# A hybrid encoder layer on one core: branch B's convolution and product placed earlier, attention's end and the first norm factor shifted

## The chip, the core and the metric

The kernel runs on one core of one Trainium2 chip. Time is device time in microseconds (us) of one execution; the median of several runs is compared. "Row" below means a line of the profile, taken of one execution by the hardware profiler. The engines are PE (TensorE matmul, with PEld its weight loads), DVE (VectorE), ACT (ScalarE), POOL (GpSimd) and SP (SyncE, which here only issues DMAs).

## The reference, cut to what matters

One layer over 1024 prompt tokens and 32 sample tokens, model width 1024, all in float32; each of five branches is 256 wide:

```python
xn = rmsnorm(x, norm1_g)
z = xn @ w_in                       # columns split among the branches
# A: gMLP
ga = gelu(za); ua = ga[..., :W]; va = layernorm(ga[..., W:], a_ln_g, a_ln_b)
oa = ua * gmlp_spatial(va, a_ws, a_bs)
# B: Conformer convolution module
b_in = zb[..., :W] * sigmoid(zb[..., W:])
b_ext = concat([hist_b, b_in])
ob = silu(layernorm(causal_dwconv(b_ext, b_conv_w) + b_conv_b, b_ln_g, b_ln_b))   # 31 taps
# C: gated short convolution (3 taps)     D: multi-scale pooling     E: cross-attention into 256 memory tokens
branches = (oa, ob, oc, od, oe)
merged = sum_n sigmoid(xn @ w_gate[n] + b_gate[n]) * (branches[n] @ w_branch[n])
x = x + merged @ w_out
x = x + (silu(hn @ w_ffn_gate) * (hn @ w_ffn_up)) @ w_ffn_down     # hn = rmsnorm(x, norm2_g)
```

`rmsnorm` divides by the root of a token's mean square. The outputs are the normed x, the memory's keys and values, and the last rows of several branches.

## The kernel before

**Layout.** Activations are feature-major: a tile has 128 features as partitions and tokens along the free axis. The tokens are two column groups `c` of 528 (two halves of 264). A float32 operand is kept as a pair of reduced-precision parts (`split`: the high part by ACT, L149, the low part by DVE, L150), and `product` (L167) makes three matmuls of each pair, so a projection of one 128-wide output tile for one group is 48 matmuls of 264 columns.

**Stages, in program order.** Memory keys and values; the query projections (which use x scaled by the norm's gain alone, `xn`); branch B's input projections; branch C's; C's gate (`gated`); A's `ua` (feature-major); A's `va` (token-major, eight tiles of 128 tokens and one of 32); branch D's input (`place`); the branch products by `branch()` for e, c, a, d, which are copied by ACT into a temporary `pb` (L1021) and written to DRAM (`pb_d`) by ACT's queue; 20 gate pairs of seven products each; the output product `wo`; the feed-forward part.

**The norm's factor.** `x_squares(c)` adds up squares of x in `r1[c]` on ACT and DVE (L370). `factors` sums them over features with matmuls to a column (`fm`, L289), takes the inverse root on ACT and DVE (`fv`, `ft`, `fr`), builds diagonal tiles (L313), and `spread` gives them back along the tokens with matmuls (`fs`, L326). `x_factor(c)` is the first half, `x_spread(c)` the second. `again` rescales x into `xs`.

**Background work.** A `runner` wraps a generator; each call with a cost steps it until the costs that it yields are used up. `att_bg` runs the attention's steps, `b_bg` runs `whole_b`: `conv_b` (30 taps on DVE and one on ACT for each of two feature halves and three token pieces: 120 taps of 512 columns, 60 of 32), then for the sample rows and each group `norm_b` (a layer norm over features: `lm`, `fm`, `fs` on PE) and `own_b` (the product of B's branch: weights `wr` loaded by SP in tiles of 128 columns, split into `wp`, twelve matmuls in two halves, copied by ACT to a temporary `pb`, L786, and written by POOL's queue). Whatever is left of `b_bg` when gate pair 15 of 20 is reached is run out at once by `b_bg.drain()`.

**What sets the order.** The framework schedules each engine's list from the program with its dependences, so a call's place decides only roughly where its instructions stand. Buffers come from pools: temporaries (`temp`) share one pool of four 528-column buffers; `by`, the convolution's accumulator, is one of them. After the attention the PSUM pool has two single banks and three double ones. In `own_b`:

```python
raw = fpool.tile([P, 2, P], F32, name=f"wr{c}_{mt}", tag="wr", bufs=1)
```

and beside the gates each of the first 16 pairs gives `b_bg` a step of 0.95 at each of its seven products.

## Time and profile before

| | us |
|---|---|
| three runs | 1716.91, 1719.30, 1724.15 |
| median | 1719.3 |
| the profiled execution | 1714.05 |
| its span on the core | 1712.0 |

| engine | busy us in the span | share |
|---|---|---|
| PE | 1655.8 | 97% |
| DVE | 1086.8 | 63% |
| ACT | 706.7 | 41% |
| POOL | 129.3 | 8% |

Times in rows are counted from the start of the span. The three runs of the table and the profiled execution are four executions of one program; the profiled one is the shortest of them.

### The profile page before, as it was taken

What the parts mean: (1) busy time and instruction counts of PE and PEld (TensorE: products, weight loads), DVE (VectorE), ACT (ScalarE), POOL (GpSimd) and SP (SyncE); (2) the same over time, 40 slices, a digit from 0 to 9 for tenths busy, and PEclk for the clock granted to TensorE, in tenths of its full rate; (3) what the DMA queues carried; (4) which work ended last, traced back from release to release, by engine and by line L of the source; (5) the groups of instructions that cost most, each with busy time, mean ns of one, the idle gap of its engine ahead of it and who ended that gap; (6) DMA issues with size and microseconds to landing.
All of it is one profiled execution on the core that took longest, in us unless ns stands there. A gap on an engine that the chain in (4) does not pass through costs nothing.

```text
span 1712.0 us, 31925 instructions
## 1 busy us (share of the span) xinstructions
PE 1655.8 (97%) x13246; PEld 1631.5 (95%) x13246; DVE 1086.8 (63%) x1946; ACT 706.7 (41%) x1314; POOL 129.3 (8%) x225
## 2 busy tenths in 40 slices
PE   8999989999999999969989999999999999999997
PEld 7999979988999999969989999999999999999997
DVE  7766674867997675535666686666666666242446
ACT  6546762555444554434443343333333334131221
POOL 1110000000111111111010000000000003000000
PEclk9999989999999999979999999999999999999999
DMA  8531102665556656635682212222222228331012
GB/s 291 171 128 43 38 13 77 223 219 207 164 159 157 147 139 166 169 109 139 201 327 82 83 38 79 84 75 88 78 85 75 75 88 300 128 110 63 29 38 102
DMA packets 77152, 213.55 MB, mean 125 GB/s; under 512 B 10544, under 2 KB 18288, under 8 KB 77008
## 3 DMA queue, kind: packets, MB, share of 16 engines
q1 hardware_dynamic: 39392, 113.80, 20.3%
q0 software_dynamic: 24848, 78.05, 15.6%
q10 hardware_dynamic: 12768, 19.67, 3.1%
q8 instruction: 103, 1.69, 0.4%
q14 instruction: 41, 0.34, 0.1%
HBM read 143.80 MB, written 67.70 MB: 124 GB/s over the span
## 4 chain that ended last, share of the span: by engine, by line
PE 80%; DMA 6%; issue 6%; DVE 4%; ACT 2%; POOL 1%; SPq 0%; ACTq 0%; POOLq 0%; DVEq 0%
PE sa L167 24%; PE dn L167 13%; PE sy L167 11%; PE z L167 9%; PE sx L167 6%; PE wo L167 5%; PE pb L167 3%; PE dq L167 2%; DMA fr<-in_w_gate 2%; PE va L167 2%; DMA pb_d<-pb 1%; DMA x<-in_x 1%; DMA mg_d<-acc 1%; PE fs L326 1%; DMA mr<-mg_d 1%
## 5 line engine op out<-in xcount | busy, mean ns | idle before, releaser
L167 PE MATMUL sa<-x,s 128*128 128x264 f32 x1968 | 252.1, 284 | 0.5 <-ACT p L1190 0.5
L167 PEld LDWEIGHTS sa<-x,s 128*128 128x128 f32 x1968 | 244.0, 188 | 0.9 <-ACT p L1190 0.7
L167 PE MATMUL dn<-hp,hl 128*128 128x264 f32 x1824 | 222.3, 284 | 0.0
L167 PEld LDWEIGHTS dn<-hp,hl 128*128 128x128 f32 x1824 | 222.1, 188 | 0.1
L149 ACT ACTIVATE s<-s 128x512 fp32r<-128x512 f32 x164 | 102.8, 631 | 143.7 <-PE sa L167 62.1
L149 ACT ACTIVATE hl<-raw 128x512 fp32r<-128x512 f32 (+1 forms) x128 | 76.8, 615 | 201.5 <-PE dn L167 130.5
L150 DVE TENSOR_TENSOR s<-s,s 128x512 fp32r<-128x512 f32 x164 | 112.4, 687 | 46.0 <-ACT s L149 45.4
L150 DVE TENSOR_TENSOR hl<-raw,hl 128x512 fp32r<-128x512 f32 (+1 forms) x128 | 84.3, 671 | 76.6 <-ACT hl L149 76.2
L167 PE MATMUL sa<-t,a 128*128 128x264 f32 x984 | 127.2, 285 | 3.2 <-DVE p L1205 3.2
L150 DVE TENSOR_TENSOR a<-fr,a 128x512 fp32r<-128x512 f32 x123 | 84.5, 688 | 71.7 <-ACT a L149 71.4
L167 PE MATMUL sy<-x,s 128*128 128x264 f32 x984 | 127.0, 285 | 0.0
L167 PEld LDWEIGHTS sa<-t,a 128*128 128x128 f32 x984 | 122.5, 189 | 4.5 <-DVE p L1205 4.5
L167 PEld LDWEIGHTS sy<-x,s 128*128 128x128 f32 x984 | 122.8, 189 | 0.0
L167 PE MATMUL z<-xs,hl 128*128 128x264 f32 x960 | 120.0, 285 | 0.5 <-ACT va_dec L841 0.5
L167 PEld LDWEIGHTS z<-xs,hl 128*128 128x128 f32 x960 | 117.9, 188 | 0.8 <-ACT va_dec L841 0.7
L149 ACT ACTIVATE a<-fr 128x512 fp32r<-128x512 f32 x123 | 77.8, 633 | 72.7 <-issue 57.8
L674 DVE SCALAR_TENSOR_TENSOR by<-b_ext,vec,by 128x512 f32<-128x512 f32 (+1 forms) x174 | 99.4, 578 | 4.7 <-ACT by L669 2.2
L167 PE MATMUL wo<-mg,hl 128*128 128x264 f32 x768 | 96.5, 288 | 3.0 <-DVE mg L150 3.0
L167 PEld LDWEIGHTS wo<-mg,hl 128*128 128x128 f32 x768 | 95.4, 191 | 3.5 <-DVE mg L150 3.5
L1436 DVE TENSOR_TENSOR y<-y,dn 128x528 f32<-128x528 f32 x40 | 28.0, 702 | 82.4 <-PE dn L167 82.3
L167 PE MATMUL pb<-br,hl 128*128 128x264 f32 x576 | 74.0, 289 | 6.3 <-ACT pb L1021 6.3
L167 PEld LDWEIGHTS pb<-br,hl 128*128 128x128 f32 x576 | 72.0, 192 | 7.4 <-ACT pb L1021 7.4
(298 smaller groups left out, 2732.7 us busy)
## 6 DMA issues: line engine op xcount, KB each, us to landing
pi<-pb_d SPq DMA_DIRECT2D x40, 528.0 KB, 5.4
fr<-in_w_gate SPq DMA_DIRECT2D x40, 512.0 KB, 4.1
pb_d<-pb ACTq DMA_DIRECT2D x64, 264.0 KB, 3.3
mg_d<-p POOLq DMA_DIRECT2D x48, 264.0 KB, 4.9
h_d<-h POOLq DMA_DIRECT2D x22, 528.0 KB, 3.0
hu<-h_d POOLq DMA_DIRECT2D x22, 528.0 KB, 8.8
fr<-in_w_fg SPq DMA_DIRECT2D x21, 512.0 KB, 3.5
fr<-in_w_fu SPq DMA_DIRECT2D x21, 512.0 KB, 3.6
```

The lines of the kernel that those rows point to most:

```text
L149: nc.scalar.activation(hl[:, 0], src, AF.Copy)
L150: nc.vector.tensor_tensor(hl[:, 1], src, hl[:, 0].bitcast(F32), op=ALU.subtract)
L167: nc.tensor.matmul(out, w(wi), rhs, start=start and i == 0, stop=stop and i == n - 1, skip_group_check=not (start and stop),)
L326: nc.tensor.matmul(ps[q][:, t0 : t0 + n] if narrow else ps[:, q, t0 : t0 + n], ones[: rows[i]], diag[: rows[i], q * Q + t0 : q * Q + t0 + ...
L674: nc.vector.scalar_tensor_tensor(dst, tap(k), col("bw", 31 * j + k), y, op0=ALU.mult, op1=ALU.add)
L1436: nc.vector.tensor_tensor(quarters(dst), quarters(dst), ps, op=ALU.subtract)
```

## The change

Seven edits stand in the diff. The first factor's `fm` and `fs` matmuls are called one product later, and those of the second group too. The attention's steps are larger (1.5 and 1.6 instead of 1.4 and 1.5), and its calls in `va` go. B's convolution gets its own buffer, is defined before branch C and is stepped beside C, `gated`, `ua`, `va` and `place`, with larger costs, and no longer beside the branches c, a and d. `own_b` loads its weights two tiles ahead and splits them one ahead, and yields less per half tile; `norm_b` is called inside it. The constants of A's layer norm and spatial bias leave the start of the program for a unit buffer that SP fills after `ua`. D's scaling moves from DVE to ACT, and the splits of a branch's parts are made for one group at a time and at later calls. The first output tile of `wo` takes the second group first.

```diff
@@ constants
-    ln_a = const.tile([P, 2, BW], F32, name="ln_a")
-    bs_b = const.tile([P, 2, P], F32, name="bs_b")
...
-        nc.sync.dma_start(ln_a[:, 0], a["a_ln_g"].partition_broadcast(P))
-        nc.sync.dma_start(ln_a[:, 1], a["a_ln_b"].partition_broadcast(P))
-        nc.sync.dma_start(bs_b, a["bs_b"])
@@ query projections, in the loop over c and j
+            if c == j == 1:
+                x_factor(0)
             if j == 0:
                 x_squares(c)
-            if c == 1:
-                (x_factor, x_spread)[j](0)
@@ branch B's projections, in the loop over j and c
             ps = projected(wb_[0], c, xn)
             if j == c == 0:
-                x_factor(1)
+                x_spread(0)
             else:
+                if j == 0:
+                    x_spread(1)
                 again()
...
             ps = projected(wb_[1], c, xn)
             if j == c == 0:
-                x_spread(1)
+                x_factor(1)
@@ conv_b, defined before branch C now, as are norm_b, own_b, whole_b and b_bg
-                y = temp("by")[:, :n]
+                y = bpool.tile([P, SEQ // 2], F32, name=f"by{j}_{t0}", tag="by")[:, :n]
...
-                    yield 0.7 if n > DEC else 0.1
+                    yield 0.9 if n > DEC else 0.15
@@ own_b
+        raws_ = {}
+
+        def load(mt):
+            if mt < KT:
+                raws_[mt] = fpool.tile([P, 2, P], F32, name=f"wr{c}_{mt}", tag="wr", bufs=2)
+                nc.sync.dma_start(
...
+        def weights(mt):
+            w = fpool.tile([P, 2, 2, P], F32R, name=f"wp{c}_{mt}", tag="wp", bufs=2)
+            split(w, raws_.pop(mt))
+            load(mt + 2)
+            return w
+
+        load(0)
+        load(1)
+        yield from norm_b(c)
+        ahead = weights(0)
+        yield
         for mt in range(KT):
...
+            w, out = ahead, temp("pb")
+            if mt < KT - 1:
+                ahead = weights(mt + 1)
...
-                yield 2
+                yield 0.9
@@ branch C, gated, ua
-                    att_bg(1.4)
+                    att_bg(1.5)
+                    b_bg(1.8)
...
-        project(gated, xs, lambda: att_bg(1.4))
+        project(gated, xs, lambda: (att_bg(1.6), b_bg(1.8)))
...
-        project(ua_evac, xs, lambda: (att_bg(1.5), b_bg(1.4)))
+        project(ua_evac, xs, lambda: (att_bg(1.6), b_bg(1.8)))
@@ after ua, and in the loop over va's tiles
+    a_const = unit(F32, "a_const")
+    ln_a, bs_b = a_const[:, :, :BW], a_const[:, :, BW : BW + P]
+    nc.sync.dma_start(ln_a[:, 0], a["a_ln_g"].partition_broadcast(P))
...
-        if i % 2 == 0:
-            att_bg()
+        b_bg(1.8)
@@ place
-        project(place, xs, lambda: (a_bg(), b_bg(2)))
+        project(place, xs, lambda: (a_bg(), b_bg(1.8)))
@@ mix_d
-                nc.vector.tensor_scalar(quarters(br[3][c][:, j]), ps, col("ds", j), None, op0=ALU.mult)
+                nc.scalar.activation(quarters(br[3][c][:, j]), ps, AF.Copy, scale=col("ds", j))
@@ beside the branches; to_parts yields after each group
-        if i == 6:
-            to_parts(2)
-        else:
-            b_bg(0.7)
+        if i in (9, 11):
+            c_parts()
+        elif i > 11:
+            b_bg(0.9)
...
-        b_bg(0.4)
+        if i in (11, 13):
+            a_parts()
...
-        if i > 3:
-            b_bg(0.4)
...
-    branch(3, lambda i: (comb(0.5), b_bg(0.4)))
+    branch(3, lambda i: comb(0.5))
@@ gates
-            hooks = {m: lambda: b_bg(0.95) for m, _ in ORDER}
+            hooks = {m: b_bg for m, _ in ORDER}
@@ wo
-        for c in range(NC):
+        for c in (1, 0) if mt == 0 else (0, 1):
```

**The first factor on PE.** In these rows z is a projection's product (here of the queries, then of branch B), `fm` the sums over features and `fs` the spread back along the tokens. PE's list before, with the start of one projection at each end:

```order
L167 MATMUL z<-xn_0_267,hl_0_302 128x264 x5
L289 MATMUL fm<-ones,r_234 128x1 x4
L167 MATMUL z<-xn_0_267,hl_0_302 128x264
L167 MATMUL z<-xn_1_270,hl_0_302 128x264 x4
L289 MATMUL fm<-ones,fc 16x1
...
L167 MATMUL z<-xn_7_288,hl_1_303 128x264 x6
L167 MATMUL z<-xn_0_235,hl_0_312 128x264 x5
L326 MATMUL fs_589<-diag,ones 128x128 x2
L326 MATMUL fs_590<-diag,ones 128x128 x2
```

PE's list after, where the first line is the end of the projection that begins the fence above:

```order
L167 MATMUL z<-xn_7_286,hl_1_298 128x264 x6
L284 MATMUL fm<-ones,r_232 128x1 x4
L284 MATMUL fm<-ones,fc 16x1
L167 MATMUL z<-xn_0_233,hl_0_307 128x264 x6
...
L167 MATMUL z<-xn_7_254,hl_1_308 128x264 x6
L321 MATMUL fs_702<-diag,ones 128x128 x2
L321 MATMUL fs_703<-diag,ones 128x128 x2
```

`fm` and `fs` each moved 43 matmuls down PE's list, and 48 stand between them in both.

**DVE between branch B's end and branch C.** Before, the last rows of B (`b_ext`), one split of weights (`hl`) and C's first rows (`c_ext`, `oc`) follow each other:

```order
L650 TENSOR_TENSOR b_ext<-z,sb_1_1140 128x512
L650 TENSOR_TENSOR b_ext<-z,sb_1_1140 128x16
L150 TENSOR_TENSOR hl_1_1226<-raw_949,hl_1_1226 128x512
L731 TENSOR_TENSOR c_ext<-z,c_ext 128x512
L731 TENSOR_TENSOR c_ext<-z,c_ext 128x16
L745 SCALAR_TENSOR_TENSOR oc_1355<-c_ext,vec,oc_1355 128x2x256
```

After, with the taps of the convolution (`by`):

```order
L647 TENSOR_TENSOR b_ext<-z,sb_1_1135 128x512
L647 TENSOR_TENSOR b_ext<-z,sb_1_1135 128x16
L150 TENSOR_TENSOR hl_1_1221<-raw_944,hl_1_1221 128x512
L671 SCALAR_TENSOR_TENSOR by_0_1443<-b_ext,vec,by_0_1443 128x512 x14
L774 TENSOR_TENSOR c_ext<-z,c_ext 128x512
L774 TENSOR_TENSOR c_ext<-z,c_ext 128x16
L671 SCALAR_TENSOR_TENSOR by_0_1443<-b_ext,vec,by_0_1443 128x512
L788 SCALAR_TENSOR_TENSOR oc_1350<-c_ext,vec,oc_1350 128x2x256
```

All 120 long taps and 60 short ones now stand ahead of the gates: 7 long ones before this place, 113 long and all the short ones between it and the last row of A's spatial product (`sp`); before, 30 long ones stood ahead of the branch products.

**PE ahead of gate pair 15.** `sy`, `sx` and `sa` are a gate pair's products, `pb<-ob,wp` those of B's branch for the second group, twelve matmuls to a tile `wp_0` to `wp_7`. Before:

```order
L167 MATMUL sy<-x_3_4550,s_15_8472 128x264 x6
L167 MATMUL pb<-ob_0_8623,wp_0_8643 128x264 x6
L167 MATMUL pb<-ob_1_8624,wp_0_8643 128x264 x6
L167 MATMUL pb<-ob_0_8623,wp_1_8666 128x264 x3
...
L167 MATMUL pb<-ob_1_8624,wp_7_8804 128x264 x3
L167 MATMUL sa<-x_0_4266,s_15_8441 128x264 x6
```

After:

```order
L167 MATMUL sa<-t_3_4639,a_14_8454 128x264 x6
L167 MATMUL pb<-ob_0_8362,wp_3_8628 128x264 x3
...
L167 MATMUL sa<-xs_0_852,a_15_8503 128x264
L167 MATMUL pb<-ob_0_8362,wp_4_8719 128x264 x3
...
L167 MATMUL pb<-ob_1_8363,wp_7_8786 128x264 x3
L167 MATMUL sa<-xs_0_852,a_15_8503 128x264 x4
L167 MATMUL sa<-xs_1_857,a_15_8503 128x264 x6
```

Before, all eight tiles of the second group stand in one block; after, tiles 0 to 3 stand among the products of the pairs ahead and 4 to 7 in the block. Both kernels' `norm_b` of a group has its `lm`, `fm` and `fs` on PE: 48 matmuls of gate products lie between each two of them where it is spread out before, and 37 and 26 after. In ACT's list 22 loads of function tables stand instead of 28; six fewer lie in `ua` and `va`.

## Rows read from the trace of the kernel before

**Rows 1.** The page's busy time by engine: us, share, instructions.

```profile
PE 1655.8 (97%) x13246; PEld 1631.5 (95%) x13246; DVE 1086.8 (63%) x1946; ACT 706.7 (41%) x1314; POOL 129.3 (8%) x225
```

**Rows 2.** PE's waits in the span, by releaser: total us, times, longest.

```profile
PE pb L167 <- ACT wp L149: 7.3, 5, 2.1
PE pb L167 <- ACT pb L1021: 6.3, 5, 3.1
PE fm L289 <- DVE bsm L694: 5.6, 1, 5.6
PE va L167 <- ACT va_all L841: 5.5, 1, 5.5
PE fm L289 <- DVE r L370: 5.0, 1, 5.0
PE wo L167 <- DVE mg L150: 3.0, 2, 2.5
PE pb L167 <- ACT ob L149: 2.5, 1, 2.5
```

**Rows 3.** Windows; columns: stretch, length, PE, PEld, DVE, ACT, POOL, clock, DMA, GB/s.

```profile
42.00:53.00 11.00, 10.45 (x61) 10.20 (x62) 7.63 (x22) 6.00 (x11) 0.00 (x0) 0.69 0.27 86
109.80:304.70 194.90, 187.17 (x1454) 178.24 (x1452) 117.89 (x269) 111.56 (x285) 0.84 (x2) 0.97 0.14 42
226.00:232.00 6.00, 0.55 (x3) 0.42 (x3) 5.93 (x12) 5.95 (x29) 0.00 (x0) 0.58 0.00 0
232.00:240.00 8.00, 8.00 (x49) 8.00 (x49) 5.18 (x13) 4.95 (x10) 0.00 (x0) 0.67 0.20 66
304.70:404.50 99.80, 91.70 (x717) 89.87 (x716) 73.77 (x113) 54.44 (x97) 4.81 (x9) 0.98 0.69 230
420.00:500.00 80.00, 79.82 (x655) 79.41 (x654) 76.62 (x133) 34.02 (x56) 9.01 (x16) 1.00 0.49 159
733.00:782.00 49.00, 32.60 (x185) 29.67 (x184) 14.84 (x33) 17.66 (x37) 5.37 (x11) 0.76 0.31 100
```

**Rows 4.** PE around the first factor, in time: start, us, instruction, wait before.

```profile
42.55 1.79 PE L289 MATMUL fm<-ones,r 128*128 128x1 f32 x8 [4.99 <-DVE r L370]
45.58 0.21 PE L289 MATMUL fm<-ones,fc 128*16 128x1 f32 x2
52.70 1.59 PE L326 MATMUL fs<-diag,ones 128*128 128x128 f32 x12
54.22 1.96 PE L167 MATMUL z<-xn,hl 128*128 128x264 f32 x14
```

**Rows 5.** The convolution's taps: DVE by form, 109.8 to 304.7; the page's group.

```profile
L674 DVE SCALAR_TENSOR_TENSOR by<-b_ext,vec,by 128x512 f32<-128x512 f32 x29 | 21.6, 744 | 0.9 <-ACT by L669 0.5
...
L674 DVE SCALAR_TENSOR_TENSOR by<-b_ext,vec,by 128x512 f32<-128x512 f32 (+1 forms) x174 | 99.4, 578 | 4.7 <-ACT by L669 2.2
```

**Rows 6.** ACT's longest wait between 304.7 and 404.5: total us, times, longest.

```profile
ACT pb L1021 <- DMA pb_d<-pb: 17.8, 11, 4.6
```

**Rows 7.** PE in time: one early norm of B, then the block before pair 15.

```profile
591.97 1.02 PE L688 MATMUL lm<-bsm,ones 128*128 128x512 f32 x2
...
739.12 1.86 PE L289 MATMUL fm<-ones,bsm 128*128 128x1 f32 x8 [5.59 <-DVE bsm L694]
...
746.06 1.05 PE L326 MATMUL fs<-diag,ones 128*128 128x128 f32 x8
...
765.24 2.20 PE L167 MATMUL pb<-ob,wp 128*128 128x264 f32 x12 [1.83 <-ACT wp L149]
769.51 3.01 PE L167 MATMUL pb<-ob,wp 128*128 128x264 f32 x12 [2.07 <-ACT wp L149]
773.30 1.73 PE L167 MATMUL pb<-ob,wp 128*128 128x264 f32 x12 [0.78 <-ACT wp L149]
```

**Rows 8.** DVE and ACT beside them, in time.

```profile
595.51 0.69 DVE L694 TENSOR_TENSOR bsm<-bsm,bsq 128x512 f32<-128x512 f32 x1
737.41 0.42 ACT L149 ACTIVATE wp<-wr 128x256 fp32r<-128x256 f32 x1 [5.51 <-DMA wr<-in_w_branch]
764.77 0.42 ACT L149 ACTIVATE wp<-wr 128x256 fp32r<-128x256 f32 x1 [0.94 <-DMA wr<-in_w_branch]
766.60 0.38 ACT L786 COPY pb<-pb 128x264 f32<-128x264 f32 x1 [1.41 <-PE pb L167]
```

More of the change, by code (lines that the diff above doesn't have):

```diff
@@ L695, in norm_b @@
         sq = None
-        yield 2
+        yield
         spread = factors([sm], BW, [(0, t, min(P, w - t)) for t in range(0, w, P)], narrow=True)[1]
         sm = None
-        yield 2
+        yield
         r = spread()[0]
@@ L714, in norm_b, with own_b, whole_b @@
                 split(dst[:, :, :, QP:], quarters(ob_s[:, j, c * 2 * QD : (c + 1) * 2 * QD]))
-            yield 2
+            yield
+    def own_b(c):
+        raws_ = {}
[3 more added lines that the diff above has]
+                nc.sync.dma_start(
+                    raws_[mt],
+                    a["w_branch"][2 + mt // 4].rearrange("p (k n) -> p k n", k=2)[:, :, mt % 4 * P : (mt % 4 + 1) * P],
+                )
+        def weights(mt):
[7 more added lines that the diff above has]
+        ahead = weights(0)
+        yield
+        for mt in range(KT):
+            w, out = ahead, temp("pb")
+            if mt < KT - 1:
+                ahead = weights(mt + 1)
+            for q_ in range(2):
+                cols = slice(q_ * Q, q_ * Q + Q)
+                ps = bank("pb")[:, :Q]
+                product(
+                    ps, [(lambda i, k=k: w[:, i, k], lambda i, k=k: br[1][c][k][:, i, cols]) for k in range(2)]
+                )
+                nc.scalar.copy(out[:, cols], ps)
+                if q_ == 1:
+                    nc.gpsimd.dma_start(pb_d[1][mt][:, c], out)
+                yield 0.9
+        br[1][c] = None
+    def whole_b():
+        yield from conv_b()
+        yield from norm_b(None)
+        for c in range(NC):
+            yield from own_b(c)
     c_ext = epool.tile([P, 2, EXT], F32, name="c_ext", tag="ext")
@@ L722, in trunk_kernel @@
     att_bg = runner(attention())
+    b_bg = runner(whole_b())
     def keep(j, c, ps):
@@ L765, in gated @@
             nc.vector.tensor_tensor(dst, ps, dst, op=ALU.mult)
-        project(gated, xs, lambda: att_bg(1.4))
-    def own_b(c):
-        for mt in range(KT):
-            raw = fpool.tile([P, 2, P], F32, name=f"wr{c}_{mt}", tag="wr", bufs=1)
-            nc.sync.dma_start(
-                raw, a["w_branch"][2 + mt // 4].rearrange("p (k n) -> p k n", k=2)[:, :, mt % 4 * P : (mt % 4 + 1) * P]
-            )
-            w = fpool.tile([P, 2, 2, P], F32R, name=f"wp{c}_{mt}", tag="wp", bufs=2)
-            split(w, raw)
-            out = temp("pb")
-            yield
-            for q_ in range(2):
-                cols = slice(q_ * Q, q_ * Q + Q)
-                ps = bank("pb")[:, :Q]
-                product(
-                    ps, [(lambda i, k=k: w[:, i, k], lambda i, k=k: br[1][c][k][:, i, cols]) for k in range(2)]
-                )
-                nc.scalar.copy(out[:, cols], ps)
-                if q_ == 1:
-                    nc.gpsimd.dma_start(pb_d[1][mt][:, c], out)
-                yield 2
-        br[1][c] = None
-    def whole_b():
-        yield from conv_b()
-        yield from norm_b(None)
-        for c in range(NC):
-            yield from norm_b(c)
-            yield from own_b(c)
-    b_bg = runner(whole_b())
+        project(gated, xs, lambda: (att_bg(1.6), b_bg(1.8)))
     TILES = [(c, q_ * Q + t0, n) for c in range(NC) for q_, t0, n in TOKENS if n == P] + [(None, 0, DEC)]
@@ L821, in trunk_kernel @@
                 )
+    a_const = unit(F32, "a_const")
+    ln_a, bs_b = a_const[:, :, :BW], a_const[:, :, BW : BW + P]
+    nc.sync.dma_start(ln_a[:, 0], a["a_ln_g"].partition_broadcast(P))
+    nc.sync.dma_start(ln_a[:, 1], a["a_ln_b"].partition_broadcast(P))
+    nc.sync.dma_start(bs_b, a["bs_b"])
     full = len(TILES) - 1
@@ L983, in to_parts @@
                 br[n][c].append(hl)
+            yield
     NAMES = ("b11", "b21", "b22", "x6", "x5", "x7", "t4")
@@ L1036, in beside_e @@
         a_bg()
-        if i == 6:
-            to_parts(2)
-        else:
-            b_bg(0.7)
+        if i in (9, 11):
+            c_parts()
+        elif i > 11:
+            b_bg(0.9)
+    c_parts, a_parts, d_parts = (runner(to_parts(n)) for n in (2, 0, 3))
     branch(4, beside_e)
     a_bg.drain()
-    del va, va_all, xd, xd_all
+    del va, va_all, xd, xd_all, a_const, ln_a, bs_b
     dwd = const.tile([P, 4, P], F32, name="dwd", tag="ws")[:, :2]
@@ L1049, in beside_c @@
     def beside_c(i):
-        if i == 4:
-            to_parts(0)
         pool_bg()
-        b_bg(0.4)
+        if i in (11, 13):
+            a_parts()
     branch(2, beside_c)
@@ L1059, in beside_a @@
     def beside_a(i):
-        if i % 2 == 1 and i < 8:
+        if i in (1, 3, 5, 7):
             mix_bg()
-        elif i == 8:
-            mix_bg.drain()
-            to_parts(3)
-        elif i > 8:
+        elif i in (9, 11):
+            d_parts()
+        elif i > 11:
             comb(0.5)
-        if i > 3:
-            b_bg(0.4)
     branch(0, beside_a)
-    branch(3, lambda i: (comb(0.5), b_bg(0.4)))
+    branch(3, lambda i: comb(0.5))
     comb.drain()
@@ L1294, in trunk_kernel @@
         w = wview(slab())
-        for c in range(NC):
+        for c in (1, 0) if mt == 0 else (0, 1):
             ps = banks2("wo")
```

## The prediction, made before the result was known

> **What bounds the kernel now.** I read the busy times first: PE 1655.8 of 1712.0 us, the next engine 1086.8 [rows 1]. Time can come off only where PE stands idle or runs slowly, so I next took PE's waits over the span [rows 2] and then cut the span into windows around them [rows 3]. The measure of a window is a full stretch: from 420 to 500 us the clock is 1.00 (2.4 GHz) and 655 matmuls pass in 80.0 us, 8.19 a us. A window that has n matmuls and lasts longer than n / 8.19 loses the difference, in waits or at the lower clock. Four places lose more than 5 us and the change touches all four: the first norm factor, the end of the attention in `va`, the branch products, and the block ahead of gate pair 15.
>
> **First factor.** PE comes to `fm` 4.99 us before `r1` has its squares, and after this wait the clock is low: 0.69 over 42 to 53 us, where 61 matmuls took 11.0 us instead of 7.4 [rows 3, 4]. The change moves `fm` and `fs` 43 matmuls down PE's list. PE was ready at 42.55 - 4.99 = 37.56; 43 matmuls at 8.19 are 5.25 us, so it reaches `fm` at 42.8, when the sum has just come (42.55). Some 0.9 us for `fm` at full clock (1.79 at half) end it at 43.7. From the end of the last `fm` (45.79) to `fs` (52.70) the old trace has 6.9 us, and nothing shows PE waiting for it, so 6.9 is an upper end of that chain: `fs` by 50.6, over by 51.4. By then PE stands 43 matmuls further than the old trace at 54.22, which is there 54.22 + 5.25 = 59.5. The gain is at most 8.1; I take **7**, as the clock may still dip at so short a wait, and 3 as the low end, the wait of 4.99 without the clock and with 2 us waited at `fs`. The second group's factor moves with it, and its sums are ready long before: nothing.
>
> **Attention and the stretch with the taps** (109.8 to 304.7 us). Here PE waits 5.5 us for the activation of a `va` tile, which stands on ACT behind attention's steps and behind table loads [rows 2]. From 226 to 232 PE does 0.55 us of work while ACT is full (5.95 of 6), and after it 49 matmuls pass in 8 us where 65.5 would, 2.0 us lost to the clock [rows 3]. With attention over before `va` both can go: PE alone could do the stretch in 194.9 - 7.5 = 187.4, and in 185 if the smaller waits (idle is 194.9 - 187.2 = 7.7 in all) go too. But the change puts the taps here. DVE has 117.9 us of work now, 22.3 of it 30 taps at 744 ns [rows 3, 5]; it gets 113 long ones, 84.1 us, and 60 short ones. The page's 174 take 99.4 us; 116 long at 744 ns are 86.3, the 58 short then 0.23 each, so 13.6 for 60. Demand: 117.9 - 22.3 + 84.1 + 13.6 = **193.3 us**, more than PE's 187. If DVE never stands still the stretch is 193 and the gain 194.9 - 193.3 = 1.6; I take **2**. Bounds: 10, if part of the taps slip behind the stretch at no cost (185); and -6, if DVE runs at 96%, as it did from 420 to 500 (76.6 of 80) while PE lost nothing: 193.3 / 0.96 = 201. The fourteen taps in a row ahead of C's first rows are 10.4 us; PE has two projections to do meanwhile, 96 matmuls or 11.7 us, and double PSUM banks, so I cost them at nothing; uncovered they would cost 10.4 once, which the rival below has.
>
> **Branch products** (304.7 to 404.5). 717 matmuls want 87.5 us and took 99.8, 12.3 lost [rows 3]. 6.3 is PE waiting for ACT's copy of `pb` [rows 2], and ACT in turn waits 17.8 us, eleven times, for an earlier `pb` to have gone to DRAM [rows 6]. `by` held one of the four temporaries; in its own buffer it leaves them to `pb`. One more buffer is one more product of 12 matmuls, 1.5 us, of slack for each of the eleven waits, whose mean is 1.6: nearly all go. DVE also loses the 22 taps or so that stood beside c, a and d. D's scaling goes to ACT, twice for each group; ACT is at 54 of 99.8 [rows 3], nothing. I take **6**; 0 if the DMAs themselves are the limit (their share is 0.69 here), 9 if the slow clock behind the waits goes too.
>
> **The block ahead of pair 15** (733 to 782). 185 matmuls want 22.6 us and took 49.0: 26.4 lost [rows 3]. The trace shows three parts: `wp` waits 5.51 for its load on ACT, which holds up the squares of the norm behind it on ACT's queue, and PE waits 5.59 for `bsm` [rows 7, 8]; then 2.5 for `ob`; then each tile of 12 matmuls takes 3.6 to 4.3 us (765.24, 769.51, 773.30) instead of 1.5, since its weights come with one load in flight. The clock is 0.76. After the change the taps are long over, four of eight tiles are spread over the pairs ahead, the norm is too, and two loads are under way. Left: for the four tiles of the block I put 2 us, of which the bound is the old pace, 4 x (3.6 - 1.5) = 8.4. For the norms: `lm` to `bsm` took 3.2 us (592.99 to 596.20) [rows 7, 8] and now has 37 matmuls, 4.5 us; `fm` to `fs` took at most 5.1 (740.98 to 746.06) and has 26, 3.2 us, so up to 1.9 for each of two or three norms, of which I put 2 in all, 4 as the bound. Gain 26 - 4 = **22**, from 14 (26.4 - 8.4 - 4) to 26.
>
> **The rest, at nothing.** `wo`'s first tile in the other order: PE waits 3.0 there for the last split, which group 1 needs later than group 0 by one DVE split; -1 to +1. SP's loads of `wr` wait for a buffer, and the gates' weight loads stand behind them in its queue; those are issued several parts ahead of their use, so 0, and the block's own bound holds what a late one would cost. `a_const` on SP waits for a unit that PE frees, with the branches' weight loads behind it, which are wanted only after `place`: 0. Six table loads fewer lie on ACT, which is not the bound.
>
> **Sum.** 7 + 2 + 6 + 22 = 37: a span of 1675, an execution of 1677 where the profiled one was 1714.05. That one lies 5 us under the median of the runs; against the median the forecast is 1719.3 - 37 = **1682**. The lower ends, 3 - 6 + 0 + 14 - 1 = 10, give 1709; the upper, 8 + 10 + 9 + 26 + 1 = 54, give 1665.
>
> **Rivals.**
> - *All of it comes* (0.12): DVE's taps fit because part of them lies where PE does not wait for DVE, and the block goes wholly: 8 + 10 + 8 + 26 = 52, 1667. For it: nobody on PE reads a tap until B's norm, long after. Against: the taps stand in one in-order queue with rows that PE does wait for.
> - *DVE becomes the bound* of the stretch (0.14): 201 us instead of 193, 8 less than forecast: 1690.
> - *The block survives* (0.09): the change does not do what it says, as four tiles still stand there. At the old pace with the norms waiting and the branches' gain gone: 7 + 2 + 0 + 14 = 23, 1696.
> - *The clock swings* (0.05). Behind each of the four idle places the granted clock fell: 0.58 at 226, 0.67 until 240, 8 us with 2.0 lost [rows 3]. If short waits for DVE do this through the stretch, some 60 us at that loss cost 15: 1697. The Trainium skill, "TensorE: Matmul & The Clock Gate", section "A second HAM failure mode: psum-queue depth-cycling", says that PE idling briefly and often between groups of matmuls makes the clock swing between its two levels, though each matmul is fast when warm. This trace has long idle followed by a low clock, and no swing under short waits; by the rule it would be 1697.
> - *Slower* (0.05): PE and DVE take turns. Attention goes from PE to DVE (maximum), ACT, PE and DVE (`pt`) and back; each DVE step now stands behind a tap of 744 ns, or fourteen. If DVE is used at 75% only, the stretch is 193.3 / 0.75 = 258, a loss of 63 against the other gains of 35: 1719.3 + 28 = 1747. It turns slower when the stretch exceeds 194.9 + 35 = 230, at 84%. Against: DVE ran at 96% beside a full PE elsewhere.
>
> **How the numbers follow.** The forecast itself has 0.55, from 1672 to 1692. With 8 in 10 held, the range is 1662 to 1706: it leaves out the slower rival and the ends of the sum. A run of this kernel can tell about 0.5% from no change: under 1710.7 is faster, over 1727.9 slower. Faster holds all the cases but the slower one and a part of the surviving block with the lower ends together: 0.89; same 0.06; slower 0.05.
>
> **What would show it.** PE's wait for `r` at the first `fm` gone and its clock full from 42 to 53; no wait for `va_all`; the stretch from the first product on `xs` to the last `sp` near 193 us with DVE over 95% busy (a busy share under 85% with new waits of PE for DVE speaks for the slower rival); ACT's wait for `pb_d` under 5 us; no `wp` waits on PE and the norm's `bsm` ready ahead of its `fm`; the block of four tiles 6 to 8 us long. Wrong would be: PE's waits by DVE's taps in branch C or attention of over 10 us, or a new wait on SP behind `wr` or `a_const`.

## The result, and the profile after

The changed kernel took 1698.1 us in the median of four runs against 1719.7 for the kernel before: a ratio of 0.9865, with a 95% interval from 0.9838 to 0.9893. The forecast was 1682, 37 us less than before; 22 came. The profiled executions stand 20.6 apart (1693.4 and 1714.05).

I cut both traces at five events that both programs have: the first product on `xs` (branch C's first), the end of the last `sp`, the first gate product, the first product of `wo` and the end of its last. Windows of the kernel before (stretch, length, busy time of PE, PEld, DVE, ACT and POOL, clock, DMA share, GB/s):

```profile
0.00:102.94 102.94, 95.62 (x688) 90.81 (x689) 79.44 (x158) 57.53 (x104) 17.57 (x39) 0.97 0.67 230
102.94:304.78 201.84, 194.11 (x1511) 185.18 (x1509) 120.92 (x275) 113.02 (x289) 0.84 (x2) 0.97 0.16 47
304.78:404.56 99.78, 91.62 (x716) 89.80 (x717) 73.71 (x114) 54.42 (x97) 4.81 (x9) 0.98 0.69 231
404.56:875.50 470.94, 451.25 (x3595) 445.09 (x3595) 323.14 (x573) 211.88 (x367) 69.58 (x103) 0.97 0.59 165
875.50:979.75 104.25, 101.21 (x816) 100.44 (x815) 68.15 (x125) 36.34 (x62) 8.33 (x17) 0.98 0.36 129
979.75:1712.00 732.25, 721.94 (x5928) 720.23 (x5927) 421.39 (x706) 233.55 (x400) 28.17 (x55) 1.00 0.26 90
```

The same of the changed kernel:

```profile
0.00:101.67 101.67, 94.11 (x688) 89.31 (x689) 80.84 (x161) 57.05 (x104) 17.46 (x39) 0.98 0.69 227
101.67:306.01 204.34, 196.60 (x1509) 187.65 (x1509) 189.87 (x421) 107.85 (x288) 0.91 (x3) 0.97 0.16 49
306.01:399.69 93.68, 89.24 (x716) 88.30 (x717) 49.77 (x79) 55.36 (x98) 4.80 (x9) 1.00 0.73 249
399.69:859.29 459.60, 447.90 (x3595) 444.86 (x3595) 279.79 (x458) 212.40 (x369) 70.00 (x103) 0.98 0.62 170
859.29:958.97 99.68, 99.34 (x816) 98.77 (x815) 65.97 (x122) 33.91 (x57) 8.33 (x17) 1.00 0.36 127
958.97:1691.50 732.53, 722.19 (x5929) 720.62 (x5927) 421.61 (x706) 233.66 (x400) 28.17 (x55) 1.00 0.26 90
```

Length by length this gives the ledger:

| stage | forecast gain | gain in the profiled pair |
|---|---|---|
| up to the first product on `xs` (first factor) | 7 | 1.3 |
| to the last `sp` (attention and taps) | 2 | -2.5 |
| branch products | 6 | 6.1 |
| gates (block ahead of pair 15) | 22 | 11.3 |
| `wo` | 0 | 4.6 |
| the rest | 0 | -0.3 |
| sum | 37 | 20.5 |

What PE waits for now, over the span of the changed kernel (total us, times, longest; the answer to [rows 2]):

```profile
PE pb L167 <- ACT pb L747: 4.8, 1, 4.8
PE z L167 <- ACT q L430: 4.4, 1, 4.4
PE fm L284 <- DVE bsm L691: 4.3, 3, 2.0
PE z L167 <- DVE c_ext L774: 3.4, 1, 3.4
PE sa L167 <- ACT a L149: 3.0, 1, 3.0
...
PE ov L564 <- DVE stats L862: 1.9, 1, 1.9
```

Five of the waits of [rows 2] are gone: for `r`, for `va_all`, for `wp` and for `ob` wholly, for `mg` nearly (0.3). The wait for the copy of a branch product fell from 6.3 to 1.4. But four new or remaining ones stand there: for the copy of a query product, for `c_ext`, for `bsm` (three times now) and for one copy of B's product. Each of the four was followed into its place and tried by an edit. A profile is one execution, and a stage's length differs from run to run also where nothing in it was edited: over the changed kernel and the runs below with the same order in it, the stretch lasted 202.7 to 204.4, the branch products 92.9 to 95.8, the gates 454.7 to 461.3 and `wo` 99.7 to 106.5. Differences within that are not read as effects.

### The profile page after: what moved, and what is told of

The parts are those of the page before. It is cut to its first block, busy times and chain, and to the rows that moved or that the text cites. A ratio compares the mean times of both kernels' runs of the same rounds, so it can differ in the third digit from the quotient of the medians.

```text
span 1691.5 us, 31928 instructions
## 1 busy us (share of the span) xinstructions
PE 1649.4 (98%) x13246; PEld 1629.5 (96%) x13246; DVE 1087.9 (64%) x1942; ACT 700.2 (41%) x1312; POOL 129.7 (8%) x225
## 4 chain that ended last, share of the span: by engine, by line
PE 83%; DVE 7%; DMA 6%; ACT 2%; issue 2%; ACTq 0%; POOL 0%; SPq 0%; DVEq 0%; POOLq 0%
PE sa L167 27%; PE dn L167 13%; PE sy L167 13%; PE sx L167 6%; PE z L167 6%; PE pb L167 5%; PE wo L167 5%; PE dq L167 2%; DVE by L671 2%; DMA fr<-in_w_gate 2%; PE fs L321 1%; PE fu L167 1%; PE fg L167 1%; DMA raw<-in_w_in 1%; DMA mr<-mg_d 1%
## 5 line engine op out<-in xcount | busy, mean ns | idle before, releaser
L167 PE MATMUL z<-xs,hl 128*128 128x264 f32 x960 | 125.5, 292 | 5.5 <-DVE c_ext L774 3.4
L167 PEld LDWEIGHTS z<-xs,hl 128*128 128x128 f32 x960 | 122.8, 196 | 6.9 <-issue 5.7
L167 PE MATMUL z<-xn,hl 128*128 128x264 f32 x576 | 72.8, 288 | 4.4 <-ACT q L430 4.4
L167 PEld LDWEIGHTS z<-xn,hl 128*128 128x128 f32 x576 | 71.7, 192 | 4.8 <-ACT q L430 4.6
```

What stands on the lines that cost most here:

```text
L167: nc.tensor.matmul(out, w(wi), rhs, start=start and i == 0, stop=stop and i == n - 1, skip_group_check=not (start and stop),)
```

## Experiments

All are edits of the changed kernel unless it is said otherwise. Their stage lengths come from windows cut at the same events.

### The new wait up to the first product on `xs`

The row of ACT ahead of PE's wait, then PE's, in the changed kernel (start, duration, instruction, idle before and its releaser):

```profile
33.70 1.15 ACT L149 ACTIVATE hl<-raw 128x512 fp32r<-128x512 f32 x2 [9.04 <-DMA raw<-in_w_in]
34.76 0.58 ACT L430 COPY q<-z 128x528 f32<-128x528 f32 x1
...
35.39 13.38 PE L167 MATMUL z<-xn,hl 128*128 128x264 f32 x96 [4.43 <-ACT q L430]
```

The copy of the first query product stands on ACT behind two splits of weights that wait 9 us for their load. In the kernel before the copy stands ahead of these splits. The factor's move didn't do that: with the factor's calls put back, ACT's list still has the splits first. Three loads of constants that the change takes out of the start stood ahead of this weight load in SP's list; without them the scheduler sets the splits before the copy. Issuing the load just ahead of it in four parts brings the old order back.

```diff
-        nc.sync.dma_start(ws_t[64:P, :, 64:P], a["ws_t"][64:P, :, 64:P])
+        for g in range(4):
+            nc.sync.dma_start(ws_t[64:P, g : g + 1, 64:P], a["ws_t"][64:P, g : g + 1, 64:P])
```

> The changed kernel with one edit: the load of ws_t's second half is issued as four DMAs instead of one, so that ACT's list has the copy of the first query product ahead of the next weights' splits again, as it stood before the change. Theory: in the changed kernel this copy stands behind two splits that wait 9.0 us for their weights (ACT idle until 33.70), PE has no free PSUM bank and waits 4.4 us, and the clock falls behind it; the wait came with the constants' loads that left the start, not with the factor's move. Then the first product on xs begins 4 to 5 us earlier (101.7 to about 97), PE's wait for the copy is gone, and the time falls by 4 to 5 us. Rival: PE only waits later for the same late data (the second group of x, or the squares at fm): the first product on xs begins less than 1.5 us earlier.

The wait for the copy is gone, and the first product on `xs` starts at 99.6 against 101.7 in the changed kernel. From the first query product on, which starts at 18.7 to 21.1, that is 80.5 us against 82.6; over all runs below it is 78.7 to 80.5 in the four with the split load and the factor's new place, and 80.4 to 83.4 in the eight that have the wait (the changed kernel among them), 2 us less in the mean. The theory had 4 to 5 and the rival under 1.5: it lies between, nearer the rival. The time was 1692.6 (ratio 0.9853, interval 0.9828 to 0.9878), within the changed kernel's interval. The second run puts the factor's calls back on top of it, those beside branch B's projections too, to price the move alone.

```diff
-            if c == j == 1:
-                x_factor(0)
...
+            if c == 1:
+                (x_factor, x_spread)[j](0)
```

> As the run before, and besides it the first factor's two halves (and the second's) are called where they stood before the change. Against that run, theory of the forecast: the move is worth 7 us (3 to 8), so PE waits some 5 us for the squares at the first fm again and the first product on xs begins about 7 us later than there (near 104). Rival: the move is worth little (under 2 us), since the group's late squares cost the same at either place.

The first product on `xs` starts at 102.0, 2.4 us later than with the move; the time was 1696.3 (0.9873, interval 0.9850 to 0.9897). PE in the run with the move:

```profile
51.01 0.94 PE L322 MATMUL fs<-diag,ones 128*128 128x128 f32 x6 [1.46 <-DVE diag L309]
...
53.16 6.10 PE L167 MATMUL z<-xn,hl 128*128 128x264 f32 x48
...
67.28 1.70 PE L322 MATMUL fs<-diag,ones 128*128 128x128 f32 x12 [1.12 <-DVE diag L309]
68.92 30.85 PE L167 MATMUL z<-xn,hl 128*128 128x264 f32 x240
```

and without it:

```profile
42.47 1.87 PE L285 MATMUL fm<-ones,r 128*128 128x1 f32 x8 [4.78 <-DVE r L366]
...
53.48 5.27 PE L167 MATMUL z<-xn,hl 128*128 128x264 f32 x41
...
67.17 34.97 PE L167 MATMUL z<-xn,hl 128*128 128x264 f32 x287
```

After the first `fs` the move leads by 41 matmuls and 0.3 us, 5.3 us in all (at 8.19 a us): the forecast's 7 less the wait of 1.5 to 1.7 for the diagonals that it had partly allowed for. By 68.92 the lead is 47 matmuls less 1.75 us, 4.0, since the second group's `fs` waits too, 1.1 us. Then 240 matmuls take 30.85 us, where the changed kernel's take 29.3: the clock is low again behind the wait (0.72 over the first 6 us). What is left is 2.4. That is one execution against one: counted from the first query product the stage is 82.8 without the move and 78.7 to 80.5 in the four runs with it, so the move is worth 2.3 to 4.0 us. In the changed kernel itself neither of these `fs` waits, since its wait for the copy brings PE there later.

### The stretch with the taps

In the changed kernel DVE is busy for 189.9 of 204.3 us. Its list around the wait for `c_ext`, then PE's wait:

```profile
107.28 10.98 DVE L671 SCALAR_TENSOR_TENSOR by<-b_ext,vec,by 128x512 f32<-128x512 f32 x14
118.17 0.77 DVE L774 TENSOR_TENSOR c_ext<-z,c_ext 128x512 f32<-128x512 f32 x2
...
130.54 4.38 DVE L489 TENSOR_TENSOR qs<-q,qs 64x528 fp32r<-64x528 f32 x6
134.94 0.77 DVE L774 TENSOR_TENSOR c_ext<-z,c_ext 128x512 f32<-128x512 f32 x2
...
135.86 8.54 PE L167 MATMUL z<-xs,hl 128*128 128x264 f32 x48 [3.40 <-DVE c_ext L774]
```

Fourteen taps in a row push C's first `c_ext` to 118.2, the attention's keys and queries behind it (8.4 us on DVE; the expectation below says 11), and so the second `c_ext` to 134.9; PE, with its double PSUM banks full, waits 3.4 us, and 48 matmuls then take 8.5 us, 2.7 more than at full clock. The edit below holds the taps back until that second `c_ext`. It also has the larger gate steps of a run further down.

```diff
-    nc.gpsimd.memset(b_ext[:, :, 0:HB], 0.0)
...
-                    b_bg(1.8)
                 evac(j, c, ps)
...
+        if j == 0 and c == 1:
+            for i in range(2):
+                nc.scalar.activation(
+                    b_ext[:, i, 0:HB], c_ext[:, 0, HC + c * 2 * QP : HC + c * 2 * QP + HB], AF.Copy, scale=0.0
+                )
```

> The run with the larger gate steps (gate stage 445.5, stretch 202.9), with the taps held back until branch C's second c_ext: the zeroing of b_ext's first columns is made by ACT from c_ext (times zero), and the convolution is not stepped beside C. In DVE's list no tap stands ahead of the attention's keys and queries then, and 28 long taps stand behind the first sp. Theory: the fourteen taps in a row push the keys and queries (11 us on DVE) and then c_ext back, which costs PE 3.4 us and 2 us of slow clock; without them the stretch is 197 to 198 and the branch stage stays at 93 to 94, as DVE has room there (49 of 91 us busy): time 5 us lower. Rival: DVE's total is what counts, and the wait comes back at sp or in the branch products: the two stages together (295.8) fall by less than 2 us.

The stretch is 199.2 against 202.9 with the larger steps alone, no wait for `c_ext` is left, and the branch products take 94.5 against 93.0: 2.2 us lower together, between the two theories (5, and under 2). The time was 1675.2 (ratio 0.9741, interval 0.9713 to 0.9770). So the stretch is 3.7 us shorter without the wait. The edit moves more than the fourteen taps, though: DVE's time for taps in the stretch falls from 101.7 to 89.0 us, and eleven long ones stand among the branch products, whose 1.5 us lie within that stage's spread. How much the attention's early end is worth was asked by undoing it alone:

```diff
-                    att_bg(1.5)
+                    att_bg(1.4)
...
+        if i % 2 == 0:
+            att_bg()
         b_bg(1.8)
```

> The changed kernel with the attention's steps and its calls in va as before the change. Theory: in the kernel before, attention inside va cost a wait of 5.5 us and about 2 us of slow clock; the stretch from the first product on xs to the last sp goes from about 203 to 209 or 210, and the time rises by 6 to 7 us. Rival: DVE with all the taps (190 us busy of 204) sets that stretch, and the wait in va is hidden by it: the stretch stays within 1.5 us of 203.

The wait in `va` is back, 5.4 us, as this row of PE's waits in that run shows:

```profile
PE va L167 <- ACT va_all L858: 5.4, 1, 5.4
```

The stretch is 207.0, 2.6 to 4.3 longer than in the runs with the early end. The waits for `stats` and `e` (1.9, 1.2 and 0.6) aren't among this run's longest ones. So the early end is worth about half of the 7.5 that its wait and its slow clock had cost. The time, 1698.8 (0.9871, interval 0.9834 to 0.9908), can't tell it from the changed kernel.

### The branch products

The forecast had the fourth temporary behind the gain of 6. One edit puts the accumulator back among the temporaries:

```diff
-                y = bpool.tile([P, SEQ // 2], F32, name=f"by{j}_{t0}", tag="by")[:, :n]
+                y = temp("by")[:, :n]
```

> The changed kernel with the convolution's accumulator back in the pool of four temporaries. In the order of DVE's list this alone spreads the taps out again (60 of 120 long ones and all the short ones then stand beside or behind D's pooling), though every call that steps the convolution stays where the change put it. Theory: the own buffer is what gave the branch products their 6 us, as ACT's copies of pb have four buffers instead of three; the branch stage goes from 93.7 back to about 99 with ACT waiting for pb_d again, and the stretch from the first product on xs to the last sp gets shorter (from 203 towards 197) since DVE has less to do there. Rival: the branch stage is faster because no tap stands on DVE beside c, a and d, and because the splits of the parts come group by group: it stays within 1.5 us of 93.7 if the taps that remain there are few, and ACT's wait for pb_d stays as it is.

The stage is 93.5 us, unchanged, and the time 1699.4 (0.9895, interval 0.9859 to 0.9931). By its length that is the rival, but the run does not decide between the two. The taps in that stage, in the kernel before and in this run (stretch, length, DVE, ACT, clock, DMA share, GB/s, of `by` alone):

```profile
304.78:404.56 99.78, 22.50 (x30) 0.82 (x1) 0.98 0.69 231
```

```profile
303.46:396.96 93.50, 0.00 (x0) 0.00 (x0) 1.00 0.72 249
396.96:859.41 462.45, 57.92 (x120) 2.31 (x4) 0.98 0.60 168
```

This run has none there: sixty long ones, two whole pieces of thirty, stand ahead of the stage, and sixty long and sixty short ones fell back beside the gates. So no accumulator is in use during the stage, and ACT's copies have all four temporaries there, as in the changed kernel. In the kernel before, one piece of thirty taps stands in the stage, and its accumulator holds one of the four. The taps' time on DVE and that temporary left the stage together, here as in the changed kernel, so the run does not rule the temporary out, as the next expectation takes it to.

The run shows two more things. Every call that steps the convolution stayed, and half of the taps moved: the accumulator's buffer decided their place. And the stretch up to the last `sp` lasted 200.0 with those taps out of it (columns as in the first windows):

```profile
103.43:303.46 200.03, 193.37 (x1510) 184.33 (x1509) 139.59 (x305) 105.74 (x284) 0.84 (x2) 0.99 0.17 49
```

DVE has 50 us less to do than in the changed kernel, and the stretch is 2.7 to 4.4 us shorter than in the runs with all the taps in it, so DVE's total does not set its length. Two other edits could still own the 6 us, the splits group by group and D's scaling on ACT. Both undone:

```diff
-        if i in (9, 11):
-            c_parts()
+        if i == 6:
+            c_parts.drain()
...
-                nc.scalar.activation(quarters(br[3][c][:, j]), ps, AF.Copy, scale=col("ds", j))
+                nc.vector.tensor_scalar(quarters(br[3][c][:, j]), ps, col("ds", j), None, op0=ALU.mult)
```

> The changed kernel with two edits undone in the branch stage: the parts of a branch are split in one call again, at the old places, and D's scaling is on DVE again. The run with the shared accumulator kept the branch stage at 93.5 us, so the fourth temporary is not what gave 6 us there; it had no tap in that stage either, where the kernel before had 30 of them, 22.5 us of DVE. Theory now: the taps' absence gave the 6 us, so the stage stays at 93 to 95 here. Rival: the splits group by group or the scaling on ACT gave them, and the stage goes back to 98 to 100.

The stage is 92.0: neither of the two edits is needed. The time was 1690.7 (0.9825, interval 0.9797 to 0.9854), not above the changed kernel's. So the 6 us go with the taps' leaving the stage, either by their 22.5 us on DVE or by the temporary that their accumulator held, and no run takes the one away without the other. ACT's wait for `pb_d` in the stage is 17.8 us before, 9.3 in the changed kernel and 9.7 and 9.1 in these two runs; nine of the eleven waits before, 13.4 us, lie between 314 and 351 us, where the thirty taps and that temporary's use lie too. The run with the taps held back comes nearest to parting them (`by` alone, columns as above):

```profile
299.78:394.28 94.50, 8.14 (x11) 0.00 (x0) 1.00 0.70 245
```

There eleven taps stand in the stage while `pb` has all four temporaries, and it lasts no longer than the spread allows. That speaks for the temporary, but with a third of the taps' time only: the cause stays open.

### The gates

What is left of the block in the changed kernel, on ACT and PE:

```profile
746.35 0.42 ACT L149 ACTIVATE wp<-wr 128x256 fp32r<-128x256 f32 x1 [5.07 <-DMA wr<-in_w_branch]
...
747.09 3.01 PE L167 MATMUL pb<-ob,wp 128*128 128x264 f32 x12 [4.75 <-ACT pb L747]
```

The loads that land in that time, in the changed kernel (736 to 750 us) and, for the block before, in the kernel before (758 to 772): KB each, median us to landing.

```profile
wr<-in_w_branch SPq DMA_DIRECT2D x2, 128.0 KB, 8.9
```

```profile
wr<-in_w_branch SPq DMA_DIRECT2D x4, 128.0 KB, 2.6
```

Two are under way instead of one, but each takes 8.9 us instead of 2.6 (over all sixteen loads of `wr` the median is 4.7 against 3.0), beside two loads of `pi` of 528 KB that weren't there in the old block's time. ACT's copies of finished halves stand behind the split that waits, so PE gets no bank. The norm, on DVE and PE:

```profile
618.89 0.69 DVE L1115 TENSOR_TENSOR s<-fr 128x512 f32<-128x512 f32 x1 [2.03 <-DMA fr<-in_w_gate]
619.62 0.69 DVE L1115 TENSOR_TENSOR s<-s,fr 128x512 f32<-128x512 f32 x1
620.23 0.69 DVE L691 TENSOR_TENSOR bsm<-bsm,bsq 128x512 f32<-128x512 f32 x1
...
620.97 1.05 PE L284 MATMUL fm<-ones,bsm 128*128 128x1 f32 x8 [1.97 <-DVE bsm L691]
```

`bsm` needs only two squares, which ACT had done by 617.5, but in DVE's list it stands behind an addition of gate weights that waits for their load. Behind both waits the clock is low (windows as above):

```profile
621.90:627.50 5.60, 5.60 (x37) 5.60 (x36) 2.39 (x10) 1.34 (x3) 0.00 (x0) 0.70 0.00 1
747.50:752.10 4.60, 4.60 (x23) 4.60 (x23) 0.42 (x1) 1.44 (x4) 1.08 (x2) 0.50 0.22 86
```

37 matmuls in 5.6 us and 23 in 4.6 want 4.5 and 2.8 at 8.19 a us: 2.9 more. The steps of `norm_b` also yield 1 instead of 2 in the changed kernel, which the list of the change leaves out. The first edit gives the work larger steps, so that nothing is left at pair 15:

```diff
-            hooks = {m: b_bg for m, _ in ORDER}
+            hooks = {m: lambda: b_bg(1.25) for m, _ in ORDER}
```

> The changed kernel with one number changed: the gate hooks give B's background work steps of 1.25 instead of 1, so that no tile of B's product is left when pair 15 is reached; in PE's list all sixteen tiles and both norms stand among the pairs ahead. Theory: what the block of four tiles still costs in the changed kernel is its wait of 4.8 us (a weight load that takes 9.4 us to land) and the slow clock behind it, about 2 us; the gate stage goes from 459.6 to about 453, the time falls by 6 to 7. Rival: the same loads, copies and splits spread among the pairs cost PE as much there: gate stage within 2 us of 459.6.

The gate stage of this run:

```profile
395.87:841.40 445.53, 443.49 (x3594) 440.93 (x3595) 279.27 (x458) 211.76 (x369) 69.94 (x103) 0.99 0.64 176
```

It is 14.1 us shorter, twice what the theory had: with the tiles spread, the `fm` of the norms no longer wait for `bsm` either. The two waits and the clock behind them, 4.8, 4.3 and 2.9, are 12.0 of it. Why `bsm` comes in time was not tried by itself; the norms stand elsewhere among the weight loads. The time was 1678.6 (ratio 0.9763, interval 0.9746 to 0.9779). The second edit prices the norm's step alone:

```diff
-        nc.vector.tensor_tensor(sm, sm, sq, op=ALU.add)
-        sq = None
         yield
-        spread = factors([sm], BW,
+        spread = factors([sm, sq], BW,
```

> The changed kernel with one DVE step of B's norm left out: the two squares are not added on DVE but summed by the fm matmuls on PE (eight small ones instead of four). In the changed kernel fm waits 4.3 us in three norms for that addition (bsm), which stands in DVE's list behind additions of weights that wait for their load (DVE idle 2.0 us for it at 618.9); the clock is low for 5.6 us behind the second. Theory: without the step fm finds its squares ready, and the gate stage goes from about 459 (459.6, 461.3, 459.4 and 456.3 in the runs with this block) to 453 to 455, the wait for the block of four tiles staying. Rival: the squares themselves (ACT) come just as late, and fm waits for them: 458 to 461.

`fm` waits 1.1 us in all instead of 4.3, and the stage is 456.5, inside the 454.7 to 461.3 of the runs with this block, so 3 us against the changed kernel and not clear of the spread. The time was 1691.2 (0.9826, interval 0.9800 to 0.9852). The 11.3 us that the change itself brought here are not only the taps' leaving: with 120 taps beside the gates again, as many as before, the run with the shared accumulator has 462.5 us, still 8.5 below the kernel before.

### `wo`

> The changed kernel with the first output tile of the product wo taken for group 0 first again, as before the change. The wo stage went from 104.3 us to 99.7 where 0 was forecast. Theory: the order did it, since group 1's last splits are needed later by one product: the stage is 104 again and the time rises by 4 to 5 us. Rival: the gain came from the end of the gates (DVE's wait for ACT there is gone), the stage stays within 1 us of 99.7.

```diff
-        for c in (1, 0) if mt == 0 else (0, 1):
+        for c in range(NC):
```

The stage is 102.0 and the time 1693.6 (0.9851, interval 0.9831 to 0.9871). That decides nothing by itself. But other runs with the changed order had 99.8, 100.5 and 105.9 in a stage that is the same code. The last of these (the first experiment) has 3.9 us of waits for `mg` in this stage, the changed kernel 0.3, and the clock is low behind the longest; PE there, and in the changed kernel:

```profile
866.03 6.22 PE L167 MATMUL wo<-mg,hl 128*128 128x264 f32 x30 [2.69 <-DVE mg L150]
```

```profile
863.45 8.77 PE L167 MATMUL wo<-mg,hl 128*128 128x264 f32 x69 [0.34 <-DVE mg L150]
```

So 4.6 us are within what this stage differs by from run to run, and not shown to be the order's.

### Put together

> The two edits that lift a wait each, together: ws_t's load in four parts (query copy ahead of the splits) and gate steps of 1.25. Theory from the single runs: the first gives 1 to 2 us up to the first product on xs (99.6 against about 100.6), the second 14 in the gate stage; no stage is touched by both: first xs at 99 to 100, gate stage 445 to 447, time 1676 to 1678. Rival: they meet somewhere (the taps' stretch starts earlier and waits longer), and the time is that of the larger steps alone or above (1678.6 or more).

This run has the four loads of `ws_t` and the steps of 1.25, on the changed kernel. First product on `xs` at 98.3, gates 443.3; the time was 1675.7 (ratio 0.9746, interval 0.9714 to 0.9779): as expected, though no clearer than 3 us from the larger steps alone. With the taps held back as well:

> The three edits that lifted a wait, together on the changed kernel: ws_t's load in four parts, gate steps of 1.25, taps held back until C's second c_ext. From the single runs' stages: first xs at 98.3 to 99.6, stretch 199.2, branches 94.5, gates 444 to 445, wo 100 to 106, the rest 732: 1669 to 1676 of span, 1674 as the time. Rival: the edits share a gain, and the time is that of the two-edit runs (1675 to 1676).

1676.7 (0.9742, interval 0.9718 to 0.9765). The stages came as expected but for the first product on `xs`, 100.4, behind queries that started late (21.1), and `wo`, 106.5: the rival as far as the time tells. And with the shared accumulator on top:

> As the run before, and the accumulator shares the pool of temporaries again. In DVE's list 60 long taps then stand ahead of the branches, none in them, and 60 long and all the short ones beside the gates. Theory: DVE is the busiest engine of the stretch up to the last sp with all taps in it (190 of 204 us), and beside the gates it has room (279 of 446 us), so taps are cheaper there: stretch 196 to 198, gates within 2 us of 445, time 1 to 3 us below the run before. Rival: taps beside the gates delay the gates' splits as in the run with the shared accumulator (gate stage 462 against 459): gates 447 to 449, time equal or above.

1680.4 (0.9760, interval 0.9735 to 0.9784). The stretch fell to 196.3 and the gates rose to 454.6: the rival, and more than it had said. The gates' DVE had room on average (279 of 446 us), but five waits of PE for `p`, the gates' sum on DVE, came to 6.5 us with the taps there, and one for a row of B's norm to 1.8.

All these beat both kernels: the larger steps alone take another 1.0 to 1.2% off the changed kernel, the versions with one or both of the other two edits lie 2 to 3 us below that, within 2 us of each other, and the last one 2 us above it.

## Why the prediction was right or wrong, point by point

**The whole.** The sign and the range (1662 to 1706) held, and three of the four signs of the terms. The forecast's own band, 1672 to 1692, did not hold. In the profiled pair the sum was 16 us too large, and it was so by two terms: the first factor (7 for 1.3) and the block (22 for 11.3). Two more were off in the pair by 4.5 each way, the taps and `wo`, and cancel; that is luck, since `wo` differs by more than that from run to run.

**First factor.** The step that failed is "The second group's factor moves with it, and its sums are ready long before: nothing." With the query copy in its old place its sums were ready, but its diagonals were not: `fs` waited 1.1 us, and the clock fell behind it. There the move is worth 2.3 to 4.0 instead of 7; in the pair compared it led by 5.3 after the first `fs`, of which the second and the clock behind it took back 2.9. In the changed kernel the new wait for `q` came on top, about 2 us in the mean. The prediction looked for new waits only at the lines that the diff moves. This one came from loads that left SP's list and let the scheduler set two splits before a copy; ACT's list shows it, and the orders read ahead of the prediction are PE's and DVE's.

**The taps.** The prediction counted its stretch from 109.8 us on. From the first product on `xs`, 6.9 us earlier, the same sums give 196 us of DVE's work and a stretch of some 200; the sign "near 193" puts the number of the one beside the start of the other. Measured were 189.9 and 204.3, with DVE 93% busy. The step that failed is "If DVE never stands still the stretch is 193": DVE's total is not what sets the length, as the run with 139.6 us of it and a stretch of 200.0 shows. PE alone wants some 194 (an estimate, the 201.8 of before less the 7.5 of its wait and slow clock). What stands above this are single waits for rows of DVE, and the largest, 3.4 us for `c_ext` with 2.7 of clock behind it, was put at nothing by "I cost them at nothing" of the fourteen taps: the 11.7 us of PE's two projections covered the taps but not the 8.4 us of keys and queries that stood behind them. Without the wait the stretch was 3.7 us shorter. The attention's early end brought about half of its 7.5 us.

**Branch products.** The size was right, 6.1 for 6. PE's wait for ACT's copies fell from 6.3 to 1.4, and ACT's for `pb_d` from 17.8 to 9.3, where "nearly all go" and under 5 were forecast. Whether the cause was right, "in its own buffer it leaves them to `pb`", is open: the temporary and the taps left the stage together, and no run takes all of one away without the other. The prediction names both and prices only the first.

**The block.** 26.4 us were there to be had, and with the larger steps the stage is 25.4 shorter than before, though not all of that is the block's: in the last run, with 120 taps beside the gates again, it is 16.3. The change got 11.3. "for the four tiles of the block I put 2 us": they cost 4.8 of wait and 1.8 of clock. That step counted two loads under way as a gain and gave no time to either, though the wait of 5.51 for a load stood in its own rows; two loads in flight of 8.9 us bring no more than one of 4.5. For the norms, "of which I put 2 in all" looked at the wrong pair: `fm` to `fs` was no wait, `lm` to `fm` was, 4.3 us, since the 3.2 us from `lm` to `bsm` were read as a length of work, where they hold a place in DVE's queue too.

**Rivals.** None of them is the result as it stands: the nearest is the surviving block (1696), by its time and by half of its mechanism. DVE as the bound by its total did not come. The slower one, PE and DVE in turns, did not come: use stayed at 93%. The clock doesn't swing through the stretch: its mean is 0.97 there, as before. The case told in the Trainium skill ("TensorE: Matmul & The Clock Gate", section "A second HAM failure mode: psum-queue depth-cycling"), in which brief and frequent idling makes it swing, would have had it lower; no run here has shown such a stretch, and each low stretch shown above followed one wait.

## What to carry to other kernels

Where a scheduler sets the order, a call's place and the place of its instructions are two things: here a buffer moved half of DVE's taps while every call stayed where it was; so read the order of every engine, also at places that the diff doesn't touch. A run that takes one thing back shows its worth only if nothing else moves with it: the accumulator that was put back among the temporaries was not in use in the stage that it was to slow. A background task that must be done by a point should be given steps that end it before that point, since the rest, run out in one block, pays waits, the clock behind them, and transfers that are all wanted at once. An engine's total work is a poor forecast of a stage's length where another engine needs single rows of it: look for those rows, and for what stands ahead of them in its list. Price a load by the traffic that it will meet.

## What was not expected of the hardware

A load of 128 KB took 8.9 us beside two of 528 KB and five of 264 KB, and 2.6 beside four of 264 KB. The stage `wo`, with the same instructions, lasted 99.7 to 106.5 us in runs whose kernels differ only elsewhere, by waits for splits (3.9 us in three, the longest 2.7, against 0.3 in the two compared above) and the clock behind them: more than most single edits here are worth. Whether the edits elsewhere or the execution set it is not shown.
